# Batched q·kT scores: four heads laid side by side on the partitions, 4 KB load runs, 16 KB store runs and 64x32 PE tiles

## The chip, the cores and the metric

One core of one Trainium2 chip. The metric is the device time of one execution in microseconds (us). The span that the profile gives is about 2 us shorter than this time. "Median" is over the timed executions of one kernel. Every ratio is the mean time of one kernel's fast runs over the mean of the earlier kernel's fast runs of the same rounds on the same chip, so it isn't quite the ratio of the medians quoted; brackets after it are a 95% interval.

## The reference

```python
# q, k: (8 batches, 8 heads, 512 rows, 64 columns), float32
def reference(q, k):
    scale = 1.0 / np.sqrt(q.shape[-1])
    return (np.einsum('bhqd,bhkd->bhqk', q, k) * scale).astype(np.float32)
```

16.8 MB are read and 67.1 MB are written, so stores are four fifths of the traffic.

## The kernel before

A head's 512 rows lie on 128 partitions, 4 rows each. So a load run is 4 x 64 floats = 1 KB, and a store run is 4 x 512 floats = 8 KB. Two heads are transposed together (their 64 columns each make 128 partitions), and the two heads' matmuls use the upper and the lower 64 rows of PE.

```python
J = S // P                                   # 4
q_r = q.rearrange("b h (p j) d -> b p h (j d)", j=J)
out_r = out.rearrange("b h (p j) k -> b p h (j k)", j=J)
# ...
for b in range(B):
    for g in range(PAIRS):                   # two heads at a time
        # ... casts of q and k to bf16 (GpSimd, first pair: ACT and DVE)
        for slab, tp in ((qb, tq), (kb, tk)):
            for j in range(J):
                nc.tensor.transpose(out=tp[:, j, :], in_=..., identity=identity)
        nc.scalar.copy(out=qT, in_=tq)
        nc.vector.tensor_copy(out=kT.rearrange("d p j -> d j p"), in_=tk)   # strided write
        o = out_pool.tile([P, 2, J * S], f32, name="o")
        for i in range(0, J, 2):
            pss = [psum_pool.tile([P, 2, S], f32, name="ps") for _ in range(2)]
            for u in range(2):
                for h in range(2):
                    rows = slice(h * D, (h + 1) * D)
                    nc.tensor.matmul(out=pss[h][:, u, :], lhsT=qT[rows, i + u, :],
                                     rhs=kT[rows].rearrange("d p j -> d (p j)"), ...,
                                     tile_position=(h * D, 0))
            for h in range(2):
                evacuate(o[:, h, i * S:(i + 2) * S], ...)     # ACT and DVE in turn
        nc.sync.dma_start(out=out_r[b, :, 2 * g:2 * g + 2, :], in_=o)
```

## Time and profile before

| | before |
|---|---|
| median (range) | 212.16 us (211.76 to 212.25) |
| span of the profiled run | 210.7 us |
| granted PE clock | not recorded (the tools print 1.0; see the profile after) |
| data packets: 1 KB loads, 8 KB stores | 16,384 and 8,192 |
| last store, landing of its 16 parts: mean, last | 206.17 and 209.73 us |

Each transfer is split over 16 DMA engines, and the trace has a landing time for each part. The transfer counts as done with the last of the 16. The mean says how much work the engines had on average; the distance from mean to last, here 3.56 us, is called the **lag** below.

### The profile page before, as it was taken

The numbers are of one execution on the slowest core, as the hardware profiler recorded it, in microseconds if no ns is written. First come the engines' busy times: TensorE is split into PE (matmuls) and PEld (weight loads), VectorE is DVE, ScalarE is ACT, GpSimd is POOL, SyncE is SP. The second block draws the span as 40 slices with busy tenths as digits, with TensorE's granted clock in tenths as the row PEclk, the third lists the DMA queues.
The fourth block names the chain that finished last, engine by engine and source line by source line (L and its number), as shares of the span: only waits on it lengthen the run. The fifth ranks groups of instructions, "written<-read, shape, count | busy, mean of one in ns | idle before, by whom it ended". The sixth has DMA issues, their size and how long they took to land.

```text
span 210.7 us, 1559 instructions
## 1 busy us (share of the span) xinstructions
PE 123.5 (59%) x512; PEld 40.5 (19%) x512; DVE 115.3 (55%) x97; ACT 84.7 (40%) x98; POOL 36.9 (18%) x68
## 2 busy tenths in 40 slices
PE   1899999897778743886148870587705877000000
PEld 0323222322232102221032210422104221000000
DVE  0699989688748940688307872178712797100000
ACT  4456666565536432446134460345503555000000
POOL 1625213300530006200070000800008000000000
DMA  6999999999999999999999999999999999999990
GB/s 185 335 357 411 428 403 425 429 426 394 401 428 425 426 382 413 428 425 423 376 425 429 426 412 386 426 431 428 398 400 426 428 428 426 428 426 428 431 409 37
DMA packets 25448, 83.99 MB, mean 399 GB/s; under 512 B 864, under 2 KB 17248, under 8 KB 17248
## 3 DMA queue, kind: packets, MB, share of 16 engines
q1 hardware_dynamic: 25440, 83.89, 99.1%
q8 instruction: 4, 0.07, 0.1%
q14 instruction: 4, 0.03, 0.0%
HBM read 16.78 MB, written 67.11 MB: 398 GB/s over the span
## 4 chain that ended last, share of the span: by engine, by line
DMA 50%; PE 8%; DVE 6%; ACT 1%; issue 0%; POOL 0%; DVEq 0%
DMA kf<-in_k_dram 50%; PE ps L101 6%; DVE kT L93 4%; DVE o L65 2%; PE tk L89 2%; ACT o L63 1%; POOL kb L81 0%; PE tq L89 0%; DVEq L65 0%
## 5 line engine op out<-in xcount | busy, mean ns | idle before, releaser
L101 PE MATMUL ps<-kT,qT 64*128 64x512 bf16 x256 | 90.1, 615 | 15.5 <-DVE o L65 5.9
L65 DVE TENSOR_SCALAR o<-ps 128x1024 f32<-128x1024 f32 x64 | 78.1, 1228 | 20.1 <-PE ps L101 18.7
L63 ACT ACTIVATE o<-ps 128x1024 f32<-128x1024 f32 x64 | 64.2, 1022 | 47.9 <-PE ps L101 47.8
L93 DVE COPY kT<-tk 128x512 bf16<-128x512 bf16 x32 | 41.3, 1291 | 39.7 <-PE tk L89 39.1
L89 PE MATMUL tq<-identity,qb 128*128 128x128 bf16 x128 | 21.6, 303 | 36.5 <-POOL qb L81 23.2
L81 POOL CAST qb<-qf 128x512 bf16<-128x512 f32 x31 | 18.2, 613 | 117.5 <-DMA qf<-in_q_dram 103.0
L92 ACT COPY qT<-tq 128x512 bf16<-128x512 bf16 x32 | 18.7, 585 | 43.5 <-PE tq L89 40.7
L101 PEld LDWEIGHTS <-qT 64*128 64x128 bf16 x256 | 16.2, 111 | 56.8 <-issue 55.9
L89 PEld LDWEIGHTS <-qb 128*128 128x128 bf16 x128 | 12.9, 131 | 56.3 <-POOL qb L81 29.6
L89 PE MATMUL tk<-identity,kb 128*128 128x128 bf16 x128 | 19.5, 307 | 3.0 <-DVE kT L93 2.5
L81 POOL CAST kb<-kf 128x512 bf16<-128x512 f32 x31 | 18.3, 613 | 7.9 <-DMA kf<-in_k_dram 3.7
L89 PEld LDWEIGHTS <-kb 128*128 128x128 bf16 x128 | 12.2, 134 | 24.0 <-issue 19.1
L81 DVE CAST kb<-kf 128x512 bf16<-128x512 f32 x1 | 0.4, 427 | 4.7 <-DMA kf<-in_k_dram 4.7
L81 ACT ACT_TABLE_LOAD x1 | 1.3, 1283 | 0.7 <-PEq L123 0.7
L81 ACT CAST qb<-qf 128x512 bf16<-128x512 f32 x1 | 0.6, 617 | 1.4 <-DMA qf<-in_q_dram 1.4
masks.py:199 POOL TENSOR_SCALAR_AFFINE_SELECT identity<-identity 128x128 bf16<-128x128 bf16 x1 | 0.3, 292 | 0.1
masks.py:197 POOL MEMSET identity<- 128x128 bf16 x1 | 0.2, 204 | 0.3 <-POOLq L123 0.3
L123 POOL MEMSET const-float32-0.0<- 128x1 f32 x1 | 0.1, 98 | 0.2 <-issue 0.2
L123 POOL MEMSET const-bfloat16-1.0<- 128x1 bf16 x1 | 0.1, 101 | 0.0
L123 POOL MEMSET const-uint8-127<- 128x1 uint8 x1 | 0.1, 101 | 0.0
L123 POOL MEMSET const-float32-1.0<- 128x1 f32 x1 | 0.1, 98 | 0.0
## 6 DMA issues: line engine op xcount, KB each, us to landing
out_dram<-o SPq DMA_DIRECT2D x32, 2048.0 KB, 19.3
qf<-in_q_dram SPq DMA_DIRECT2D x7, 1024.0 KB, 26.0
kf<-in_k_dram SPq DMA_DIRECT2D x7, 1024.0 KB, 27.5
qf<-in_q_dram SPq DMA_DIRECT2D x4, 256.0 KB, 4.3
kf<-in_k_dram SPq DMA_DIRECT2D x4, 256.0 KB, 4.6
```

Source lines behind the costliest of these rows:

```text
L63: nc.scalar.mul(out=dst, in_=src, mul=scale)
L65: nc.vector.tensor_scalar(out=dst, in0=src, scalar1=scale, scalar2=None, op0=mybir.AluOpType.mult)
L81: copy(out=dst.rearrange("p j h d -> p h j d"), in_=slab[:, 2 * g:2 * g + 2, :].rearrange("p h (j d) -> p h j d", j=J))
L89: nc.tensor.transpose(out=tp[:, j, :], in_=slab[:, j].rearrange("p h d -> p (h d)"), identity=identity)
L92: nc.scalar.copy(out=qT, in_=tq)
L93: nc.vector.tensor_copy(out=kT.rearrange("d p j -> d j p"), in_=tk)
L101: nc.tensor.matmul(out=pss[h][:, u, :], lhsT=qT[rows, i + u, :], rhs=kT[rows].rearrange("d p j -> d (p j)"), start=True, stop=True, tile_p ...
L123: nc = _bacc.Bacc("TRN2", target_bir_lowering=False, num_devices=1)
```

## The change

The intent is fewer and larger packets. Four heads lie side by side, 32 partitions each with 16 rows: a load run is 4 KB, and the store of 8 rows is 16 KB. The price is paid on PE: the heads of a column block have different k, so each matmul becomes four with 32 output columns each, and transposes are made per half. The copy of k to bf16 now puts its columns in order by reading PSUM with a step, not by writing with a step.

```diff
-    q_r = q.rearrange("b h (p j) d -> b p h (j d)", j=J)
-    out_r = out.rearrange("b h (p j) k -> b p h (j k)", j=J)
+    q_r = q.rearrange("b (x g) (m j) d -> b (g m) x (j d)", x=2, j=R)       # R = 16, G = 4, M = 32
+    out_r = out.rearrange("b (x g) (m j) k -> b x (g m) j k", x=2, j=R)
 ...
-        step = 2 if b == 0 else H
-        for h in range(0, H, step):
-            nc.sync.dma_start(out=qf[:, h:h + step, :], in_=q_r[b, :, h:h + step, :])
-            nc.sync.dma_start(out=kf[:, h:h + step, :], in_=k_r[b, :, h:h + step, :])
+        nc.sync.dma_start(out=kf, in_=k_r[b])
+        nc.sync.dma_start(out=qf, in_=q_r[b])
 ...
+                for j in range(JB):                                        # JB = 8
+                    for x in range(2):
+                        nc.tensor.transpose(out=tp[x * D:(x + 1) * D, j, :],
+                                            in_=slab[:, x, j0 + j, :], identity=identity)
 ...
-            nc.vector.tensor_copy(out=kT.rearrange("d p j -> d j p"), in_=tk)
+                    nc.vector.tensor_copy(out=kT[:, :, j0:j0 + JB],
+                                          in_=tp.rearrange("d j p -> d p j"))
 ...
-                    for h in range(2):
-                        nc.tensor.matmul(out=pss[h][:, u, :], lhsT=qT[rows, i + u, :],
-                                         rhs=kT[rows].rearrange("d p j -> d (p j)"), ...)
+                    for g in range(G):
+                        cols = slice(g * M, (g + 1) * M)
+                        for x in range(2):
+                            nc.tensor.matmul(out=pss[x][cols, u, :],
+                                             lhsT=qT[rows, j0 + j + u, cols],
+                                             rhs=kTg[rows, g, :], ...,
+                                             tile_position=(x * D, g * M))
```

The buffers for casts, transposed tiles and outputs were also resized (3, 3, 7 to 2, 2, 6), the PSUM tiles of the transposes went from one buffer to two, and all casts now run on GpSimd.

## The prediction

> **What bounds the kernel now.** I read the engine table first, then the DMA lines, then the busy time by stretch, then single rows of the timeline.
>
> ```profile
> PE 123.5 (59%) x512; PEld 40.5 (19%) x512; DVE 115.3 (55%) x97; ACT 84.7 (40%) x98; POOL 36.9 (18%) x68
> ...
> q1 hardware_dynamic: 25440, 83.89, 99.1%
> q8 instruction: 4, 0.07, 0.1%
> ```
>
> No compute engine is above 59%, while the data queue fills 99.1% of 16 DMA engines' span. The stretches (times, busy time of PE, PEld, DVE, ACT, POOL with counts, granted clock, DMA share, GB/s) say it more sharply:
>
> ```profile
> 0.00:2.00 2.00, 0.00 (x0) 0.00 (x0) 0.00 (x0) 1.27 (x1) 0.70 (x6) 1.00 0.05 17
> ...
> 4.00:8.00 4.00, 2.62 (x16) 1.40 (x17) 1.74 (x2) 1.24 (x3) 1.84 (x3) 1.00 1.00 310
> 8.00:20.00 12.00, 12.00 (x50) 3.32 (x47) 10.71 (x9) 7.79 (x9) 5.86 (x10) 1.00 1.08 373
> ...
> 100.00:180.00 80.00, 46.58 (x194) 15.92 (x193) 44.57 (x38) 31.78 (x37) 13.88 (x24) 1.00 1.03 416
> 180.00:204.00 24.00, 0.00 (x0) 0.00 (x0) 0.00 (x0) 0.00 (x0) 0.00 (x0) 1.00 1.01 427
> 204.00:206.00 2.00, 0.00 (x0) 0.00 (x0) 0.00 (x0) 0.00 (x0) 0.00 (x0) 1.00 0.72 303
> 206.00:207.00 1.00, 0.00 (x0) 0.00 (x0) 0.00 (x0) 0.00 (x0) 0.00 (x0) 1.00 0.16 66
> 207.00:209.00 2.00, 0.00 (x0) 0.00 (x0) 0.00 (x0) 0.00 (x0) 0.00 (x0) 1.00 0.06 25
> ```
>
> Compute ends before 180 us; stores alone then drain for 24 us at 427 GB/s. Loads alone (4 to 8 us) reach only 310 GB/s with the engines just as full. And from 207 to 209 us the share is 0.06, one engine of sixteen: fifteen have finished by about 207 us, one ends at 209.4 us.
>
> Which engine is that? The instruction queue moved four blocks (0.07 MB). In the stretch 20 to 30 us one of them is
>
> ```profile
> q8 instruction: 1, 0.02, 0.6%
> ```
>
> 0.6% of 16 engines x 10 us is 0.96 us, during which 15 data packets are in flight, not 16. Following the packet records back to back, the engine that carries the block at 167.6 us is the one that ends at 209.4 us. Fifteen engines end at 205.5 us on average, so it is 3.9 us late, and four blocks of 0.96 us are 3.8 us. So I take it that all four go through one DMA engine, and that this engine sets the end.
>
> **What the Trainium skill says.**
> 1. "DMA: Bandwidth & Descriptors", Queues, rings and completion order: each DMA engine takes its descriptors in ring order. The trace agrees with the late engine: it doesn't catch up. Its section Where 436 GB/s comes from gives a ceiling of 435 GB/s; this trace shows 427 for 8 KB packets.
> 2. "Runtime: NRT & Kernel Launch", Instruction fetch mechanics: instructions are refilled in 16 KiB blocks of 256. The trace agrees: 512 + 512 PE rows are four times 256, and four blocks came, 257 PE rows apart.
> 3. "TensorE: Matmul & The Clock Gate", Part 3, Measured speedup vs the span model: 16 small tiles ran 10.6 times as fast as one after the other. This trace shows two row tiles side by side, and no run yet shows column tiles. Four matmuls, of which one takes 615 ns, took 1.03 us in all: the two of a pair start 10 to 30 ns apart, and pairs follow at 427 ns.
> 4. "SBUF — State Buffer", The DMA port swizzle: an access pattern that crosses to a new 16-byte line at each step pays. The k copy (8-byte step in what it writes) takes 1291 ns for 512 columns, while the eviction takes 1228 ns for 1024; so strided is about twice as dear per column here. The rows for points 3 and 4 (start, duration; then busy us, mean ns):
>
> ```profile
> 23.32 1.03 PE L101 MATMUL ps<-kT,qT 64*128 64x512 bf16 x4
> ...
> L65 DVE TENSOR_SCALAR o<-ps 128x1024 f32<-128x1024 f32 x64 | 78.1, 1228 | 20.1 <-PE ps L101 18.7
> ...
> L93 DVE COPY kT<-tk 128x512 bf16<-128x512 bf16 x32 | 41.3, 1291 | 39.7 <-PE tk L89 39.1
> ```
>
> **The change part by part.**
> DMA packets: 16,384 load packets of 1 KB become 4,096 of 4 KB; 8,192 stores of 8 KB become 4,096 of 16 KB. Costs: stores at 427 GB/s over 16 engines are 16 x 8192 / 427 = 307 ns each. An average engine works from 1.8 to 205.5 us = 203.7 us; its 512 stores take 157.2 us, leaving 46.5 us for 1,024 load packets, 45.4 ns each. A line through (1024 B, 45.4) and (8192 B, 307) has 8.0 ns per packet and 36.5 ns per 1000 bytes (estimate). Hence 4 KB: 157.5 ns, 16 KB: 606 ns. An engine then has 256 x 157.5 + 256 x 606 = 40.3 + 155.1 = 195.4 us: minus 8.3 us. This is the gain that the change is made for.
>
> PE instructions: transposes double (512, each half as wide), matmuls go from 256 to 1,024; with their weight loads 3,074 rows in place of 1,026. So 12 blocks in place of 4: 8 more x 0.96 = 7.7 us more on the engine that ends last. The average engine doesn't see it.
>
> The start: before, the first loads are 256 KB pieces, the first copies run on ACT and DVE, and the first store is issued at 12.2 us, while loads keep the queue full to about 21 us. After, all of k of batch 0 (1 MB at some 400 GB/s, 2.6 us, plus 0.7 us to be seen) lands at 5.2 us, q at 7.8. GpSimd casts k0, q0, k1, q1 in that order, 1.2 us each (twice 613 ns): k1 ends at about 10.2 us. Then 16 transposes (0.9 to 1.7 us at 107 ns each, as pairs or one by one), a k copy (1.2 to 2.5 us), the same again, then q's: first matmul at 15 to 19 us. Four steps of 2.3 us (a row of matmuls 1.2, eviction 1.02, hand-over) fill the first 2 MB: first store at 24 to 28 us. Loads issued ahead of it, now seven of 1 MB, last until 1.8 + 7.34 MB / 402 GB/s = 20 us. So the DMA stands idle for 4 to 8 us; I take 5.
>
> Sum for the last engine: 1.8 + 195.4 + 11.5 (12 blocks) + 5 + 1.3 (last packet to end of span) = 215.0, less 1 for blocks that fall into the idle stretch: span 214.0. Adding the 1.5 us between span (210.7) and time (212.2) gives 215.5 us. Check on the kernel before: 1.8 + 203.7 + 3.8 + 1.3 = 210.6.
>
> Compute: evictions stay 64 + 64. A step is 2.3 us, eight a batch 18.5 us. In the later batches the 64 transposes stand in one block ahead of the matmuls, with only two transpose buffers: 5 us if transposes pair and the k copy costs 1.2 us, 9 us if neither. So 23.5 to 27.5 us a batch against 24.4 us of DMA (25.9 for the late engine). Before, a batch took 16.4 us (4.09 us a head pair). The slack is gone, but six output buffers of 2 MB cover a bubble of that size, so I let DMA remain the bound.
>
> **The rivals.**
> A. Plain gain: the blocks don't matter (spread over engines, or another engine), the start idles little. Span 1.8 + 195.4 + 4 + 2 = 203, time about 205. For it: DMA is the bound, and the packets do get bigger. Against it: the stretch 207 to 209 us.
> B. As in the sum: gain, fetches and start cancel, 212 to 218 us.
> C. Compute becomes the bound: 17 + 3 x 20 + 5 x 26 + 10 (last two stores) = 217, up to 228 us with dear k copies. For it: 2.3 us steps with three PSUM buffers for two outputs; against it: DVE is 55% busy and the k copy may be halved.
> D. Column tiles run one after the other: 512 pair slots x 427 ns = 219 us on PE plus 55 us of transposes, 280 us or more. The skill's figure is against it; I give it 5%.
> E. 16 KB runs are cut, or the 32 KB step between partitions in memory slows the writes: up to 2.3 us more than B, or worse.
>
> **Range and chances.** A about 20%, B about 45%, C and E about 30%, D 5%. B straddles the limit of 2% (216.4 us). So: predicted 215.5 us, 8 times in 10 between 204 and 228; faster by over 2% 0.22, within 2% 0.38, slower 0.40.
>
> **What would show it.** The DMA table should have some 8,200 data packets, share of the span below 95%, and the instruction queue 12 blocks. The GB/s row should dip near 20 to 27 us, then stand above 420 in the middle. At the end one engine should work alone (share 0.06) for some 8 to 11 us. The k copy should stand at 1.2 to 2.5 us for 1,024 columns; eight matmuls should start within 0.2 us. I am wrong if the middle shows holes in the DMA row (C), if the tail is no longer than now (A), if matmuls of different columns start 427 ns apart (D), or if a pure-store stretch shows below 427 GB/s (E).

## The result, and the profile after

| | before | after |
|---|---|---|
| median, same rounds | 211.97 us | 211.70 us (211.47 to 212.18) |
| ratio | | 0.999 [0.9967, 1.0012] |
| span of the profiled run | 210.7 us | 209.8 us |
| last store's 16 parts: mean | 206.17 us | 203.76 us |
| last store's 16 parts: last | 209.73 us | 209.01 us |
| lag (last minus mean) | 3.56 us | 5.25 us |

The time didn't move: a loss of 1.6% was predicted, and the difference is a tenth of a per cent the other way. The mean engine is done 2.4 us earlier, the last one only 0.7 us.

The page of the kernel after, first the engines, then the clock row, then the queues:

```profile
PE 126.8 (60%) x1536; PEld 42.3 (20%) x1536; DVE 93.5 (45%) x80; ACT 80.8 (38%) x81; POOL 33.1 (16%) x38
...
PEclk9999999965555555575558555576555855555555
...
q1 hardware_dynamic: 8960, 83.89, 95.6%
q8 instruction: 12, 0.20, 0.3%
```

The packets fell to 8,960 (8,192 with data and 768 of under 512 B) and the instruction blocks rose from 4 to 12, both as predicted; the queue's share, 95.6%, was forecast below 95%. PE has three times the rows at nearly the same busy time.

The clock row shows about half the clock after the first 44 us. That doesn't make the changed kernel's PE the slower one. The page of the kernel before has no clock row at all, so its 1.0 is no measurement, and its matmuls are long throughout (shortest, median and longest in ns, between 60 and 75 us):

```profile
L101 PE MATMUL ps<-kT,qT x30: 580/627/631, 61.2 to 74.3; 64*128 64x512 bf16 x30
```

The kernel of experiment 4 below has matmuls of the same shape and does have a clock row: their median is 374 ns between 17 and 40 us, where it grants 1.0, and 617 ns between 140 and 185 us, where it grants 0.5 nearly all the time. By their durations, then, the matmuls of the kernel before ran as at half clock from start to end (602 to 632 ns between 8 and 20 us), and the changed kernel has a fast stretch that the kernel before lacks. The Trainium skill, "TensorE: Matmul & The Clock Gate", Part 1, says that the clock is gated by how busy PE has been. This agrees only in part: the fast stretch, 16.5 to 43.8 us, is the changed kernel's busiest, but the kernel before shows none, although its PE is busy for all of 8 to 20 us. The run with only half the PE rows (experiment 4) shows the same mean clock (0.635 against 0.637), so the small tiles aren't what sets it.

The stretches of the kernel after (same columns as in the prediction: PE, PEld, DVE, ACT, POOL busy, clock, DMA share, GB/s):

```profile
4.00:8.00 4.00, 0.42 (x2) 0.18 (x2) 0.00 (x0) 0.00 (x0) 1.04 (x1) 1.00 1.03 423
20.00:21.00 1.00, 0.98 (x23) 0.34 (x24) 1.00 (x2) 0.82 (x1) 0.70 (x1) 1.00 0.34 127
21.00:22.00 1.00, 1.00 (x33) 0.59 (x22) 1.00 (x2) 0.46 (x1) 0.00 (x0) 1.00 0.67 283
...
100.00:180.00 80.00, 55.12 (x596) 17.28 (x592) 35.46 (x31) 31.02 (x32) 12.17 (x12) 0.56 1.01 428
...
190.00:200.00 10.00, 0.00 (x0) 0.00 (x0) 0.00 (x0) 0.00 (x0) 0.00 (x0) 0.50 1.01 431
200.00:202.00 2.00, 0.00 (x0) 0.00 (x0) 0.00 (x0) 0.00 (x0) 0.00 (x0) 0.50 0.92 393
202.00:204.00 2.00, 0.00 (x0) 0.00 (x0) 0.00 (x0) 0.00 (x0) 0.00 (x0) 0.50 0.42 180
204.00:206.00 2.00, 0.00 (x0) 0.00 (x0) 0.00 (x0) 0.00 (x0) 0.00 (x0) 0.50 0.13 57
206.00:208.00 2.00, 0.00 (x0) 0.00 (x0) 0.00 (x0) 0.00 (x0) 0.00 (x0) 0.50 0.08 33
```

Loads alone now reach 423 GB/s where they had 310; the middle went from 416 to 428. So the gain is there. From 20 to 22 us the DMA has little to do: 0.66 + 0.33 = 1.0 us by these two rows, 1.3 us by the packet records. In the middle there is no hole, so PE at half clock and the longer transpose block cost nothing: the DMA is still the bound. At the end 393 GB/s at 200 us shows that the first engines are done, and from 204 us on only one to two of 16 work.

The start and the matmul tiles, from the timeline (start, duration) and then the groups (busy us, mean ns). The first row is the first matmul, the last the first store's issue:

```profile
14.96 1.80 PE L104 MATMUL ps<-kT,qT 64*32 64x512 bf16 x24
...
19.14 0.61 PE L104 MATMUL ps<-kT,qT 64*32 64x512 bf16 x8 [0.17 <-DVE o L67]
...
20.84 2.02 SPq L112 DMA_DIRECT2D out_dram<-o  x2
```

```profile
L104 PE MATMUL ps<-kT,qT 64*32 64x512 bf16 x1024 | 95.9, 527 | 38.4 <-ACT o L65 20.4
L67 DVE TENSOR_SCALAR o<-ps 128x1024 f32<-128x1024 f32 x64 | 75.2, 1219 | 75.7 <-DMA out_dram<-o 57.6
...
L89 DVE COPY kT<-tp 128x1024 bf16<-128x1024 bf16 x16 | 19.0, 1218 | 15.4 <-PE tp L86 15.4
```

Eight small matmuls take 0.61 us together where one has a mean of 527 ns: all eight tiles of the array work side by side. The k copy takes 1218 ns for 1,024 columns read with a step, as long as the eviction that reads its 1,024 in order. And DVE's idle time ahead of the eviction is ended mostly by a store that gives its buffer back (57.6 of 75.7 us): DVE waits for the DMA, not the other way round.

### The profile page after: what moved, and what is told of

It reads as the page before. It is cut to its first block, busy times and chain, and to the rows that moved or that the text cites. A ratio compares the mean times of both kernels' runs of the same rounds, so it can differ in the third digit from the quotient of the medians.

```text
span 209.8 us, 3444 instructions
## 1 busy us (share of the span) xinstructions
PE 126.8 (60%) x1536; PEld 42.3 (20%) x1536; DVE 93.5 (45%) x80; ACT 80.8 (38%) x81; POOL 33.1 (16%) x38
## 3 DMA queue, kind: packets, MB, share of 16 engines
q1 hardware_dynamic: 8960, 83.89, 95.6%
## 4 chain that ended last, share of the span: by engine, by line
DMA 64%; DVE 14%; PE 5%; POOL 2%; ACT 1%; issue 1%; SPq 0%; DVEq 0%; POOLq 0%
DMA out_dram<-o 45%; DMA kf<-in_k_dram 15%; DVE o L67 12%; PE ps L104 4%; DMA qf<-in_q_dram 3%; DVE kT L89 2%; PE tp L86 2%; ACT o L65 1%; POOL kb L77 1%; POOL qb L77 0%; SPq L51 0%; SPq L112 0%; DVEq L67 0%; POOLq L77 0%
## 5 line engine op out<-in xcount | busy, mean ns | idle before, releaser
L104 PE MATMUL ps<-kT,qT 64*32 64x512 bf16 x1024 | 95.9, 527 | 38.4 <-ACT o L65 20.4
L67 DVE TENSOR_SCALAR o<-ps 128x1024 f32<-128x1024 f32 x64 | 75.2, 1219 | 75.7 <-DMA out_dram<-o 57.6
L104 PEld LDWEIGHTS <-qT 64*32 64x32 bf16 x1024 | 17.7, 99 | 105.7 <-issue 100.4
L77 POOL CAST kb<-kf 128x1024 bf16<-128x1024 f32 x16 | 16.3, 1043 | 90.2 <-DMA kf<-in_k_dram 68.8
L92 ACT COPY qT<-tp 128x1024 bf16<-128x1024 bf16 x16 | 15.9, 1013 | 35.6 <-PE tp L86 35.4
L89 DVE COPY kT<-tp 128x1024 bf16<-128x1024 bf16 x16 | 19.0, 1218 | 15.4 <-PE tp L86 15.4
L86 PE MATMUL tp<-identity,kb 128*64 128x128 bf16 x256 | 17.0, 280 | 12.9 <-POOL kb L77 12.7
L77 POOL CAST qb<-qf 128x1024 bf16<-128x1024 f32 x16 | 16.3, 1043 | 37.6 <-DMA qf<-in_q_dram 37.5
L86 PE MATMUL tp<-identity,qb 128*64 128x128 bf16 x256 | 16.6, 287 | 5.2 <-POOL qb L77 2.6
L86 PEld LDWEIGHTS <-kb 128*64 128x64 bf16 x256 | 12.6, 147 | 22.6 <-POOL kb L77 17.7
L86 PEld LDWEIGHTS <-qb 128*64 128x64 bf16 x256 | 13.0, 153 | 11.7 <-POOL qb L77 7.0
```

Source lines behind the costliest of these rows:

```text
L67: nc.vector.tensor_scalar(out=dst, in0=src, scalar1=scale, scalar2=None, op0=mybir.AluOpType.mult)
L77: nc.gpsimd.tensor_copy(out=dst[:, x].rearrange("p j d -> p (j d)"), in_=slab[:, x])
L86: nc.tensor.transpose(out=tp[x * D:(x + 1) * D, j, :], in_=slab[:, x, j0 + j, :], identity=identity)
L89: nc.vector.tensor_copy(out=kT[:, :, j0:j0 + JB], in_=tp.rearrange("d j p -> d p j"))
L92: nc.scalar.copy(out=qT[:, j0:j0 + JB, :], in_=tp)
L104: nc.tensor.matmul(out=pss[x][cols, u, :], lhsT=qT[rows, j0 + j + u, cols], rhs=kTg[rows, g, :], start=True, stop=True, tile_position=(x * ...
```

## The experiments

Two things were to be tested: what the packets give, and what the PE rows take. The theory after the result: the packets give about 5 us to every engine; the tripled PE rows take about 3 us from the engine that ends last; about 1 us is lost at the start. The rivals: the packets give nothing (the layout in memory takes it back); the rows are innocent, and the half clock or the start is what costs.

### 1. Undo the loads: 1 KB runs again

```diff
-    q_r = q.rearrange("b (x g) (m j) d -> b (g m) x (j d)", x=2, j=R)
+    q_r = q.rearrange("b h (p j) d -> b p h (j d)", j=4)
-        nc.sync.dma_start(out=kf, in_=k_r[b])
+        nc.sync.dma_start(out=kf.rearrange("p x (c f) -> p (x c) f", c=4), in_=k_r[b])
```

(q's load and k's pattern likewise. The result is wrong, as rows lie in other places.)

> The changed kernel with the loads of the kernel before (1 KB runs, same number of transfers, same bytes; the numbers come out wrong on purpose, since the rows land elsewhere). If 4 KB runs are worth what the line through the packets said, 6.2 us per engine are lost: about 218 us. By the landing times of the two traces the loads gained 5 us: about 216.7 us. If the packets gained nothing that reaches the end: 211.7 us.

Measured: 215.85 us (215.23 to 215.93), ratio 1.0163 [1.0146, 1.0181]. The load stretch, 1 KB runs:

```profile
4.00:8.00 4.00, 0.34 (x2) 0.18 (x2) 0.00 (x0) 0.00 (x0) 1.04 (x1) 1.00 1.09 361
```

361 GB/s in place of 423 with the same transfer sizes. Against the changed kernel this is 0.017 in the ratio, or some 3.7 us: what the loads' longer runs are worth at the end of the run. On the average engine they are worth more, because the longer loads also fill the hole at 20 to 22 us (DMA share 1.1 there). Its packets take 204.3 us in this run by the records, instruction blocks left out, against 198.5 us in the changed kernel: 5.8 us, near the 6.2 us of the prediction's line.

### 2. Undo the stores: 8 KB runs again

```diff
-            os = [out_pool.tile([P, JB, S], f32, name="o") for _ in range(2)]
+            os = [out_pool.tile([P, 2, 4 * S + 8], f32, name="o") for _ in range(2)]
-                nc.sync.dma_start(out=out_r[b, x, :, j0:j0 + JB, :], in_=os[x])
+                nc.sync.dma_start(out=out_r[b, x, :, j0:j0 + JB, :].rearrange("p (c j) k -> p c (j k)", c=2),
+                                  in_=os[x][:, :, 0:4 * S])
```

The gap of 8 floats in the tile cuts each run in two; the result is right.

> The changed kernel with padded output tiles, so that each store is cut into 8 KB runs (same stores, same order, right result). By the line of the prediction 16 KB runs are worth 2.1 us per engine: about 213.8 us. By the spacing of packets in the traces (608 against 2 x 305.6 ns) 0.8 us: 212.5 us. If nothing: 211.7 us.

Measured: 213.35 us (212.65 to 214.44), ratio 1.0055 [1.0029, 1.0082]; 0.0065 over the changed kernel, 1.4 us. A pure-store stretch:

```profile
190.00:200.00 10.00, 0.00 (x0) 0.00 (x0) 0.00 (x0) 0.00 (x0) 0.00 (x0) 0.50 1.01 426
```

426 GB/s against 431 with 16 KB. Both undone parts together are 5.1 us at the end, so the packets do give about 5 us there, and the rival that they give nothing falls. On the average engine the 8 KB stores cost 2.9 us (201.3 against 198.5 us, one profiled run each), so the two parts are 8.7 us there.

### 3. The kernel before with its matmuls cut in four

```diff
-                        nc.tensor.matmul(out=pss[h][:, u, :], lhsT=qT[rows, i + u, :], ...,
-                                         tile_position=(h * D, 0))
+                        for c in range(0, P, 32):
+                            nc.tensor.matmul(out=pss[h][c:c + 32, u, :], lhsT=qT[rows, i + u, c:c + 32], ...,
+                                             tile_position=(h * D, c))
```

> The kernel before, with each matmul cut into four of 32 columns: the data transfers, their order and the evictions stay, the PE rows go from 1026 to 2562, so ten instruction blocks in place of four. Theory of the prediction (all blocks go through the one DMA engine that ends last): 6 more blocks x 0.96 us = 5.8 us, about 217.7 us. Rival R1, read from the landings of the changed kernel (each block holds up another DMA engine, so the cost is divided by sixteen): 0.4 us more on the average engine, at most about 1 us at the end, 212.0 to 213.0 us. Rival R2 (the PE work itself is hidden in any case): no change of either kind.

Measured: 214.97 us (214.83 to 215.15), ratio 1.0126 [1.0108, 1.0144]; correct. So 1,536 more PE rows (768 matmuls and their weight loads) cost 2.7 us without the new layout and without the new start. This page has no clock row either; its matmuls take 579 to 632 ns, as in the kernel before. The result lies between what the theory (5.8 us) and R1 (about 1 us at most) expected, and neither is met. The landing mean went to 208.08 us and the lag to 4.3 us: the rows cost the average engine 1.9 us and the last one 0.8 us more.

### 4. The changed kernel with one matmul in place of four

```diff
-                    for g in range(G):
-                        cols = slice(g * M, (g + 1) * M)
-                        for x in range(2):
-                            nc.tensor.matmul(out=pss[x][cols, u, :], lhsT=qT[rows, j0 + j + u, cols],
-                                             rhs=kTg[rows, g, :], ..., tile_position=(x * D, g * M))
+                    for x in range(2):
+                        nc.tensor.matmul(out=pss[x][:, u, :], lhsT=qT[rows, j0 + j + u, :],
+                                         rhs=kTg[rows, 0, :], ..., tile_position=(x * D, 0))
```

Wrong (all four heads see one k); loads, stores and evictions are as in the changed kernel.

> The changed kernel with one matmul of 64x128 in place of the four of 64x32 (wrong numbers on purpose): PE rows 3074 to 1538, blocks 12 to 6, all transfers as they were. Theory of the prediction: 6 x 0.96 = 5.8 us less, about 206 us. Rival R1 (blocks go round the engines): 0.4 to 1 us less, 210.7 to 211.3 us. Rival R2: 211.7 us. The granted clock of PE, 0.64 in the changed kernel and 1.0 before, should go back towards 1.0 if it is the number of small tiles that lowers it.

Measured: 208.43 us (208.06 to 208.90), ratio 0.9821 [0.9803, 0.9839]. Its end:

```profile
200.00:202.00 2.00, 0.00 (x0) 0.00 (x0) 0.00 (x0) 0.00 (x0) 0.00 (x0) 0.50 1.01 434
202.00:204.00 2.00, 0.00 (x0) 0.00 (x0) 0.00 (x0) 0.00 (x0) 0.00 (x0) 0.50 0.33 139
204.00:206.00 2.00, 0.00 (x0) 0.00 (x0) 0.00 (x0) 0.00 (x0) 0.00 (x0) 0.50 0.04 16
```

All engines work until 202 us and nearly nothing is left at 204. Landing mean 203.31 us, last 205.61: the mean is only 0.45 us earlier than in the changed kernel, the last 3.4 us. So most of the packets' gain reaches the end when the rows are gone, at the same mean clock: the rival that the clock is what costs falls too. The time lies between the 206 us of the prediction's theory and the 210.7 to 211.3 us of R1, and neither is met.

### 5. The same rows, without their work

To separate the count of rows from what the small tiles read, three tiny matmuls of 4 columns were added for each real one, to the kernel before and to the one of experiment 4:

```diff
+                        for _ in range(3):
+                            nc.tensor.matmul(out=pss[h][:, u, 0:4], lhsT=qT[rows, i + u, :],
+                                             rhs=kT[rows].rearrange("d p j -> d (p j)")[:, 0:4], ...)
                         nc.tensor.matmul(out=pss[h][:, u, :], lhsT=qT[rows, i + u, :], ...)
```

> The kernel before with three extra matmuls of 4 columns (and their weight loads) ahead of each real one, on the same PE tile: PE rows 1026 to 2562 as in the run with the cut matmuls, so again ten instruction blocks, but only a quarter of its extra reading from SBUF (3 x 128 weight columns a matmul in place of 3 x 512 moving columns). If the 2.7 us that the cut matmuls cost came with the number of PE rows: again 2.5 to 3 us more than before, about 215 us. If it came with PE's reading of SBUF beside the stores: a quarter, 0.7 us, about 213 us.

> The kernel with one 64x128 matmul in place of four (wrong numbers on purpose; it was 3.3 us faster than the changed kernel), given three tiny matmuls of 4 columns for each, so 3074 PE rows again with little reading. If rows (and their blocks) are what costs: back to 211 to 212 us. If it is the reading of moving columns: it stays at 208.5 to 209.3 us.

Measured: on the kernel before 214.50 us (213.83 to 215.46), ratio 1.0113 [1.0087, 1.0138], as dear as cutting the real ones; it is correct. On experiment 4 (wrong, like it) 212.05 us (212.02 to 212.82), ratio 1.0004 [0.9984, 1.0025]: 3.6 us more by the medians (3.9 by the ratios), back to the time of the changed kernel. Its end:

```profile
202.00:204.00 2.00, 0.00 (x0) 0.00 (x0) 0.00 (x0) 0.00 (x0) 0.00 (x0) 0.50 0.48 205
204.00:206.00 2.00, 0.00 (x0) 0.00 (x0) 0.00 (x0) 0.00 (x0) 0.00 (x0) 0.50 0.13 57
206.00:208.00 2.00, 0.00 (x0) 0.00 (x0) 0.00 (x0) 0.00 (x0) 0.00 (x0) 0.50 0.08 33
```

The tail of the changed kernel is back, to the digit in its last two rows. So the cost comes with the added rows, and not with the 64x32 tiles or the columns that they read. PE's busy time rose with the rows, from 123.9 to 140.0 us, and the two aren't told apart here.

### 6. Is it the instruction blocks on one engine, as predicted?

This needs no new run. If all 12 blocks went through one engine, one engine would be late and fifteen even. Counting, in the changed kernel's landing times, the engines that are more than 0.5 us behind the median one:

```
block fetched at (us)     29.1   36.5   44.0   58.4   76.4   91.0
next transfer lands at    32.0   37.0   46.8   60.8   77.9   95.0
engines over 0.5 us late     2      3      4      5      6      7
```

After each block one more engine is late, by 0.8 to 1.5 us when it first shows. A block takes 0.88 to 1.03 us of one engine, and each of these went to another one. That isn't all: after each of the 12 blocks the next data packet is long too, 0.99 to 1.02 us for 16 KB, where the median is 0.61, and 0.44 us for 4 KB, where it is 0.16. So a block costs its engine about 1.2 to 1.4 us.

The one engine that ends last has something else as well: its lag grows in small steps, 1.8 us at 76 us, 2.5 at 101, 3.7 at 145, 5.2 at 175, and stands still once compute has ended. The packet records show where. One step, near 153 us, is an 8 KB block of the second instruction queue (q14) that takes 0.31 us of this engine, and the packet after it takes 0.91 us. Much of the rest is spread over its data packets: of the 392 packets of 16 KB that start between 165 and 180 us, 18 take over 616 ns, and by their back-to-back times 17 of these are on this one engine (619 to 680 ns, in place of 611). After 185 us, with compute over, 1 of 476 does.

### 7. More of the dose on the kernel before

```diff
-                        for _ in range(3):
+                        for _ in range(6):
```

(against the variant of experiment 5 on the kernel before)

> The kernel before with six tiny matmuls ahead of each real one in place of three: 4098 PE rows, 16 blocks. Three cost 2.4 us. If the cost goes with the rows: 4.8 us more than before, about 217 us. If it was a single step (one unlucky engine): about 214.5 us.

Measured: 230.38 us (229.67 to 231.82), ratio 1.0857 [1.0831, 1.0884]; correct. A miss as a test of the dose:

```profile
PE 158.8 (70%) x2048; PEld 86.1 (38%) x2048; DVE 118.2 (52%) x97; ACT 86.2 (38%) x98; POOL 36.9 (16%) x68
...
GB/s 187 351 349 424 400 409 429 393 291 310 376 430 423 375 332 417 426 347 353 322 428 430 414 345 379 427 424 413 323 386 429 424 390 334 411 211 298 282 413 279
```

The GB/s row has holes down to 291 and 211: compute couldn't feed the stores any more, so another limit took over.

### 8. Any engine's rows, or PE's?

```diff
                 for x in range(2):
                     evacuate(os[x][:, j:j + 2, :], pss[x])
+                for _ in range(12):
+                    nc.vector.memset(tiny_v, 0.0)
+                    nc.gpsimd.memset(tiny_g, 0.0)
```

(against experiment 4; wrong, like all variants of it)

> The kernel with one whole 64x128 matmul for four small ones (wrong on purpose, 208.43 us, ratio 0.982, 6 blocks) with 768 tiny memsets more on VectorE and 768 on GpSimd: as many rows more as the 1,536 tiny matmuls that took it to 212.05 us (ratio 1.000), but none on PE. Both added engines stay under 75 per cent busy, the work of PE, the loads and the stores is unchanged. If any executed row costs (its instruction block must be fetched, and something per row slows one DMA engine), the block count rises from 6 to about 12, and the time to 211 to 212.5 us, ratio 0.995 to 1.003, with the last landing about 5 us over the mean of the 16 engines. If only PE's rows cost, 208 to 209.2 us, ratio 0.980 to 0.987, with the last landing about 2.3 us over the mean. In between (209.5 to 210.5): the blocks explain a part, and the rest is PE's own.

Measured: 257.05 us (256.95 to 257.33), ratio 1.2123 [1.2095, 1.2152]. Another miss, and the chain of waits and the groups say why:

```profile
POOL 38%; issue 25%; DVE 23%; PE 5%; DMA 3%; ACT 1%; DVEq 1%; SPq 0%; POOLq 0%
...
L113 POOL MEMSET tiny_g<- 128x4 f32 x768 | 78.9, 103 | 43.0
```

The casts stand in GpSimd's order behind the memsets of the batch before them, so it set the pace. VectorE alone was tried next, together with half the dose of tiny PE matmuls (384 of them, so 768 rows with their weight loads):

```diff
 # vector rows: as above, without the line of nc.gpsimd
 # half dose on PE, against experiment 5:
-                        for _ in range(3):
+                        for _ in range(3 if u == 0 else 0):
```

> The kernel with 1,538 PE rows (208.43 us, ratio 0.982) with 768 tiny memsets more on VectorE (62 ns each, 48 us in all, VectorE at some 68 per cent). GpSimd is left alone, so the DMA should stay the bound and its row show no hole after 25 us. If any executed row slows the late DMA engine: half of the 3.6 us of 1,536 PE rows, ratio 0.989 to 0.993, late engine 3.5 us or more over the mean. If only PE's rows do: ratio 0.980 to 0.985, late engine about 2.3 us over the mean.

> The same kernel with 384 tiny PE matmuls more, that is 768 PE rows more with their weight loads, half of what took it from ratio 0.982 to 1.000; 9 instruction blocks. If the cost is proportional to PE's rows: ratio 0.989 to 0.993 (about 210.2 us), the late engine some 3.6 us over the mean. If it comes in a step (a threshold of rows or of PE's busy time): either 0.980 to 0.985 or 0.997 to 1.002.

Measured: VectorE 210.76 us (210.23 to 212.45), ratio 0.9965 [0.9925, 1.0005]; half dose on PE 210.61 us (210.04 to 212.06), ratio 0.9947 [0.9913, 0.9981]. The half dose lies between none (0.9821) and the full one (1.0004), at two thirds of the way, just outside the expected range, with an interval that reaches down to half: no step, and roughly proportional. (In both runs four of the six times lie between 210.0 and 210.8 us and two between 211.8 and 212.5; what parts them is open.) VectorE's time can't be read in the same way, because its DMA did have a hole late on:

```profile
170.00:180.00 10.00, 7.01 (x46) 2.43 (x44) 6.00 (x63) 4.99 (x5) 0.00 (x0) 0.50 1.01 431
180.00:184.00 4.00, 1.75 (x4) 0.21 (x4) 3.58 (x10) 0.84 (x1) 0.00 (x0) 0.50 0.78 330
184.00:188.00 4.00, 3.53 (x10) 0.66 (x10) 2.71 (x22) 2.23 (x3) 0.00 (x0) 0.50 0.85 356
```

In such a hole the late engine catches up (its lag falls from 3.8 to 2.3 us here). But its lag up to there can be read, in one profiled run of each:

| variant of experiment 4 | lag at about 76 us | at about 145 us | at about 184 us |
|---|---|---|---|
| no added rows | 1.8 us | 1.6 us | 2.3 us |
| 768 rows on VectorE | 1.6 us | 2.2 us | 3.8 us |
| 768 rows on PE | 1.7 us | 2.7 us | 3.9 us |
| 1,536 rows on PE | 1.6 us | 3.5 us | 5.0 us |

By 184 us rows on VectorE put 1.5 us on the late engine, and as many rows on PE 1.6 us. So, as far as one profile of each can show it, it isn't a matter of PE alone: executed rows of either engine do it. That they do it in the same way isn't shown. With VectorE two steps, when transfers at 131 and 158 us take this engine 0.7 and 0.6 us longer than usual, fall together with 8 KB blocks of the second instruction queue, which fetched 9 blocks here and 3 without added rows; with PE one such step does, of 0.7 us at 152 us.

### 9. Can the late engine be relieved?

```diff
             for x in range(2):
+                if b == B - 1 and j0 == JB and x == 0:
+                    for p0, p1 in ((0, 120), (120, 128)):
+                        nc.sync.dma_start(out=out_r[b, x, p0:p1, j0:j0 + JB, :], in_=os[x][p0:p1])
+                    continue
                 nc.sync.dma_start(out=out_r[b, x, :, j0:j0 + JB, :], in_=os[x])
```

The Trainium skill, "DMA: Bandwidth & Descriptors", Why a DMA increments its semaphore by 16 and not by 1, says that the number of engines is the largest up to 16 that divides the dimension, so 15 for 120 partitions, and that the lowest-numbered ones are used. If the late engine were the sixteenth, it would be spared one share.

> The changed kernel with one store of the last pair cut into 120 + 8 partitions: by the skill's account of how a transfer is shared out (page on DMA, number of engines k), the first part runs on engines 0 to 14 and the second on 0 to 7, so engine 15 has 4.9 us less to do. If the one late engine is number 15 and it sets the end: 2.5 to 3 us less, about 209 us. If it is 8 to 14: no change, 211.7 us; if 0 to 7: 0.6 us more.

Measured: 215.85 us (215.74 to 216.64), ratio 1.0181 [1.0158, 1.0205]; correct. In the last store one part landed at 197.94 us, the mean was 205.97 and the last 212.80. So one engine was indeed left out, and the late one was another. The cut itself was dear:

```profile
190.00:200.00 10.00, 0.00 (x0) 0.00 (x0) 0.00 (x0) 0.00 (x0) 0.00 (x0) 0.50 0.99 352
```

352 GB/s in place of 431 at nearly the same DMA share; an engine less explains only 431 x 15/16 = 404. None of the three expected outcomes came, and the rest of the loss stays open.

### 10. The start

First loads in halves, first casts on DVE and ACT:

```diff
-        nc.sync.dma_start(out=kf, in_=k_r[b])
+        step = 1 if b == 0 else 2
+        for x in range(0, 2, step):
+            nc.sync.dma_start(out=kf[:, x:x + step], in_=k_r[b, :, x:x + step])
 ...
-                nc.gpsimd.tensor_copy(out=dst[:, x]..., in_=slab[:, x])
+                copy = first if b == 0 else nc.gpsimd.tensor_copy
+                copy(out=dst[:, x]..., in_=slab[:, x])
```

> The changed kernel with the first loads in halves and the first casts on DVE (k) and ACT (q) in place of GpSimd; all else the same, 3074 PE rows. In the changed kernel the DMA stood idle for 1.3 us at 20 to 22 us, before the first store. If that idle time reaches the end: about 1.3 us less than the changed kernel, 210.4 us. If the late DMA engine sets the end and uses the idle stretch to catch up: no gain, 211.7 us.

Measured: 212.20 us (210.98 to 213.16), ratio 0.9991 [0.9956, 1.0025]; correct. The first store was issued at 18.87 us, 2.0 us earlier, but:

```profile
18.00:19.00 1.00, 1.00 (x23) 0.50 (x21) 0.94 (x1) 0.84 (x1) 0.26 (x1) 1.00 0.06 25
```

The hole only moved forward, because a load that had been queued ahead of the first store now came after it. By the packet records the DMA is idle for 2.0 us between 17 and 26 us here, and for 1.3 us in the changed kernel.

### 11. Versions that try to have both

Two heads side by side instead of four: 64 partitions each, 8 rows, so 2 KB loads and still 16 KB stores, whole 128x128 transposes, two matmuls for one where the changed kernel has four; 1,538 PE rows instead of 3,074. The first loads are halved and the first casts spread as in experiment 10. The second version mixes: k loaded as in the changed kernel (4 KB), q and the output in the two-head layout.

```diff
-    G = H // 2
-    JB = 8
+    G = 2
+    Y = H // (2 * G)
-    q_r = q.rearrange("b (x g) (m j) d -> b (g m) x (j d)", x=2, j=R)
+    q_r = q.rearrange("b (a g) (m j) d -> b (g m) a (j d)", g=G, j=R)      # R = 8
-    out_r = out.rearrange("b (x g) (m j) k -> b x (g m) j k", x=2, j=R)
+    out_r = out.rearrange("b (a g) (m j) k -> b a (g m) j k", g=G, j=R)
-                    for x in range(2):
-                        nc.tensor.transpose(out=tp[x * D:(x + 1) * D, j, :], ...)
+                    nc.tensor.transpose(out=tp[:, j, :],
+                                        in_=slab[:, j].rearrange("p x d -> p (x d)"), identity=identity)
```

> A version meant to beat both: two heads side by side, 64 rows each with 8 rows a partition: 2 KB load runs, 16 KB store runs, 64x64 PE tiles, 1538 PE rows, six blocks; the first loads in halves, and the first casts on DVE and ACT. Against the changed kernel: 1.2 us lost on load packets (256 to 512 of 83 ns an engine), some 3 us won on PE rows, up to 1.3 us won on the idle DMA before the first store. About 209 us, 1.2 to 1.8% faster than before. If PE rows cost nothing: about 212 us.

> k in the layout of four heads (4 KB runs), q and the output in that of two (2 KB loads, 16 KB stores): 1538 PE rows as in the version with two heads, and some 0.7 us less in k's load packets than there. About 209.2 us, 1.3% faster than before; if the packets of k don't matter any more, as the version with two heads, 209.9 us.

Measured: two heads 209.96 us (208.80 to 210.61), ratio 0.9885 [0.9856, 0.9913]; mixed 210.67 us (210.41 to 211.12), ratio 0.9928 [0.9913, 0.9942]; both correct. The end of the two-head version:

```profile
200.00:202.00 2.00, 0.00 (x0) 0.00 (x0) 0.00 (x0) 0.00 (x0) 0.00 (x0) 0.50 0.61 262
202.00:204.00 2.00, 0.00 (x0) 0.00 (x0) 0.00 (x0) 0.00 (x0) 0.00 (x0) 0.50 0.10 41
```

Its first store is issued at 16.43 us, and the records show no idle stretch at 20 to 22 us. It beats both kernels by about 1.1%, the best correct version found, so 2 KB loads suffice here. How much of this is rows and how much the start isn't separated. The mixed version is slower, although half of its loads are longer: by the records its DMA is idle for 1.6 us between 17 and 26 us.

## Why the prediction was wrong

**The step that failed** is "So I take it that all four go through one DMA engine, and that this engine sets the end", and with it the term of 11.5 us for 12 blocks on one engine. That four blocks of 0.96 us matched the 3.9 us of the late engine was a coincidence, and the reading that the block at 167.6 us sits on the last engine was wrong in the trace of the kernel before itself: over the transfer that this engine moves at that time (landing at 170.5 us) its lag goes only from 3.43 to 3.56 us, while at the next landing four engines and no longer three are over 1 us behind the median. Twelve blocks came, at the predicted size, but they stop one engine after another (experiment 6): 12 x 0.94 / 16 is 0.7 us on the average engine, 1.0 us with the long packet after each. The lag that they should have raised by 7.7 us rose from 3.56 to 5.25, by 1.7 us.

The terms of the sum beside what they measured, in the profiled run:

| term | predicted | measured |
|---|---|---|
| first packet | 1.8 us | 2.5 us (other runs of this layout 1.8) |
| packets, average engine | 195.4 us | 198.5 us |
| idle DMA after the start | 5 us | 1.3 us, and 0.3 us near 53 us |
| blocks | 11.5 us on the last engine, less 1 | 0.7 us on the average engine |
| lag of the last engine, beyond its blocks | none | 5.25 us |
| last packet to end of span | 1.3 us | 1.2 us |
| span | 214.0 us | 209.8 us |

(Packets measured: the records' busy time per engine is 199.2 us, less 0.7 us of blocks. The column of measured terms adds up to 209.8.)

**The packets** were right in direction and in form. Between the two kernels the average engine gained 4.9 us, not 8.3 (203.6 less 0.2 of blocks before, 198.5 after, where 195.4 was expected). At their best the packets are as estimated: 8 x 608 ns in a pure-store stretch against 606 predicted, and a median of 159 ns for 4 KB against 157.5. But their means over the whole run are 618 and 163.5 ns. Undone one at a time in the changed kernel, the loads and the stores cost the average engine 5.8 and 2.9 us, 8.7 us in all and near the predicted 8.3, and 5.1 us of them reached the end. Why the same packets give 3.8 us less between the two kernels isn't settled; that 4.9 and 5.1 us agree is no proof of either.

**The start** was too dark: the first matmul came at 15.0 us, at the early end of the predicted 15 to 19, and the first store at 20.8 instead of 24 to 28. The four steps took 5.9 us, not 9.2. The matmuls of a step took 1.1 to 1.6 us (waits within a step left out), no less than the 1.2 expected, but the timeline shows them beside the evictions of the step before, not after them. The k copy was at the cheap end of its range.

**The PE rows do cost** about what was feared in kind, not in size: 2.4 to 2.7 us for 1,536 rows on the kernel before, 3.6 us on the changed one without its small tiles. In the changed kernel nearly all of that is on the engine that ends last (+3.4 us at the last landing, +0.45 us at the mean), as the prediction had it; the cause given for it was wrong. On the kernel before it is the other way round: the cut matmuls cost 1.9 us at the mean and 0.8 us of lag (experiment 3), where the prediction said that the average engine doesn't see them.

**The rivals.** C (compute becomes the bound) and D (column tiles one after the other) fell: no hole from 100 to 180 us, and eight tiles in 0.61 us. E (16 KB runs are slow) fell: 431 GB/s. The truth lies between A and B: gain 4.9 us on the average engine, of which 0.5 us go to more blocks, 1.3 us are lost to idle DMA at 20 us, 0.7 us to a later first packet in that run, and 1.7 us to the lag; which leaves 0.7 us at the last landing (209.73 to 209.01).

**What stays open** is what slows the one late DMA engine as rows are executed. Shown is that its lag rises with rows of PE and of VectorE, about 1.5 us for 768 more, that it stops rising when compute stops, and that in the changed kernel it comes from data packets that are a little longer on this engine alone, and from one instruction block (experiment 6). The trace shows no other transfer that would lengthen these packets. Each of these executions, the timed ones too, yields a span and a granted clock, so each was recorded; whether the recording of rows is itself what loads that engine can't be told from these runs. Nor is it settled why the kernel before, with a third of the changed kernel's rows, has a lag of 3.56 us, where experiment 4, with half of them, has 2.30. The number of packets isn't the reason: experiments 1 and 2, with 21,248 and 13,056 packets at the changed kernel's rows, have lags of 4.95 and 4.06 us, not more than its 5.25 with 8,960.

## What to carry to other kernels

In a kernel whose bound is the DMA, look at the last landing engine by engine: the mean tells what the packets are worth, the lag tells what something else takes back. Larger runs are worth their price only if they don't multiply the executed rows; here half the rows with 2 KB loads beat both 1 KB and 4 KB loads. And a product that happens to equal an observed gap (four blocks, four microseconds) is no evidence until a second prediction of it, here "which engine is late after each block", has been checked in the same trace. Lastly, a clock column that reads 1.00 where the page has no clock row says nothing: compare the durations of equal matmuls.

## What the Trainium skill lacked or had wrong

- "Runtime: NRT & Kernel Launch", Instruction fetch mechanics, calls the cost of crossing a 16 KiB block "mostly hidden". No run here tests this for the engine that executes; but with the DMA as the bound each block takes a DMA engine 0.88 to 1.03 us of its data time, and the data packet after it takes some 0.4 us longer in the changed kernel (0.28 us for 4 KB).
- No page says which DMA engine fetches the blocks: here a different one for each block that could be followed (from two to seven late engines over six successive blocks).
- No page has the cost of executed rows to a DMA-bound kernel: 1,536 more PE rows took 2.4 to 3.6 us, and 768 memsets on VectorE put 1.5 us on the late DMA engine, about as much as 768 PE rows (1.6 us).
- "DMA: Bandwidth & Descriptors", Latency and other measured facts, has engines 7 and 15 as usually slower and guesses at the descriptor rings of GpSimd's transfers. All transfers here are issued by SyncE, and one engine is late all the same, by 2.3 to 5.3 us in the kernels that the DMA bounds (experiment 9 apart); that experiment shows that it isn't the one that a 120-partition store leaves out. The trace doesn't number the engines, so 7 stays possible.
- No page gives the rate of a store that is cut so that it runs on 15 engines: 15/16 of 431 would be 404 GB/s, and 352 were measured (experiment 9).
- "PSUM — Partial Sum Buffer", Specifications, warns of patterns that aren't contiguous, for matmuls. For a VectorE read of PSUM with a step no price showed: 1218 ns for 1,024 bf16 columns, against 1219 ns for a contiguous f32 eviction of the same width. (No contiguous bf16 copy by VectorE was run to compare.)
